# Per-head sums of the recurrent layer: sixteen 64x64-stationary products on four quarters of the array in place of four 128x128-stationary ones

## The chip, the cores and the metric

One core of a Trainium2 chip runs the whole program. The metric is the device time of one execution in microseconds (us). The engines work side by side, each through its own list of instructions in a fixed order: TensorE (PE in the profile; its weight loads are PEld), VectorE (DVE), ScalarE (ACT), GpSimd (POOL) and SyncE (SP, which here only issues DMAs). An instruction whose input is not ready holds up everything behind it on its engine.

## The reference, cut to what matters

The program is two layers over 512 tokens of width 1024. The first has an RWKV-7 time mixer with 12 heads of 64 channels beside a cross-attention into 256 memory tokens; the second has chunked attention. Both end in a gated feed-forward part. Two places of the first layer need one number per token and head:

```
kk = k_h * per_head(k_k)
kk = kk / jnp.maximum(jnp.sqrt(jnp.sum(kk * kk, axis=-1, keepdims=True)), 1e-12)
...
y = wkv7_scan(r_h, w_h, k_h, v_h, -kk, kk * a_h)
mean = jnp.mean(y, axis=-1, keepdims=True)
var = jnp.mean(jnp.square(y - mean), axis=-1, keepdims=True)
y = (y - mean) * lax.rsqrt(var + LN_X_EPS) * per_head(lnx_w) + per_head(lnx_b)
```

The sum runs over the 64 channels of a head. Everything is float32.

## The kernel before, in words

Tensors lie transposed: channels on the 128 partitions, 512 tokens along the free axis. The 12 heads are worked on as 6 pairs, one head on partitions 0 to 63 (`HS[0]`), the other on 64 to 127 (`HS[1]`). A pair `i` passes through three generators:

- `prepare(i)` projects keys, queries and values with products against weight tiles (the helper `dense`, lines L241, L242 and L245: the high and low parts of activations by `whi`, then `wlo`). Its inner generator `keys()` squares the keys, calls the helper for the norm, multiplies (L1195 to L1204 build the tiles `AR` and `KB`), forms the scores (L1210), copies them to `Lc` (L1215) and sends them through DRAM (L1218, L1224) to `Lr`, from which a triangular solver on DVE (L1233 to L1246) works.
- `front(i)` and `back(i)` turn the scores into the state recursion and the outputs, mostly with small products of 64 or 32 rows (L1300, L1324, L1326, L1358, L1375, L1418, L1434, L1445, L1453, L1462, L1467, L1472). `back` calls the helper for the output norm.

The helper is `head_rsqrt`. It is called by `keys()` for pairs 0, 1, 4 and 5 and by `back` for pairs 0, 3, 4 and 5, eight calls in all; the other pairs use `head_wide`, which is not touched. A call holds the squares `sq` (128 channels by 512 tokens) stationary in four pieces of 128x128 and passes the two columns of `sel` through them (L1082). `sel` has a column for each head, with zeros in the other head's rows. So each piece yields 128 tokens by 2 heads in one PSUM bank. DVE then adds or clamps a constant (`fix`, its line is that of the caller: L1192 for keys, L1487 for outputs), takes ten small steps of a reciprocal root (`rsqrt_steps`, L280 to L284), spreads the result (L1088), and PE turns it back (L1091).

The generators of several pairs, the memory keys and values of both layers (`mem_kv`, products L241 to L245 with 256 columns, and L1060 to L1062) and other work are woven into one program by `weave`: it takes the next step from the generator that is furthest behind, by the cost in ns that each step yields. A scheduler then orders each engine's list with its own estimates of durations. So a yielded cost or the number of instructions can change the order of instructions that the diff does not touch. Weight tiles come in by SP (L214 into `wraw`, two buffers), ACT makes `whi` (L195) and DVE or a DMA the rest `wlo` (L203, three buffers each).

Small products share four PSUM banks that are handed out in turn (`ps_s`); the memory products have two others (`psl`) and the projections two more (`psd`).

Of the kernel before, what the change touches and what calls it, by code (L numbers as in the profile page):

```python
# [18 lines left out]
P = 128  # L19
# [102 lines left out]
def trunk_kernel(ctx, tc, A, out):  # L122
    nc = tc.nc
    PE, V, SC, GP = nc.tensor, nc.vector, nc.scalar, nc.gpsimd
# [34 lines left out]
    def C(name, lo=0, n=None):  # L159
        o, w = COFF[name]  # L160
        return cst[:, o + lo:o + lo + (w if n is None else n)]
# [23 lines left out]
    def tmp(dt=F32, shape=(P, S)):  # L185
        return banks["tmp"].tile(list(shape), dt, name="tmp", tag="tmp")
# [43 lines left out]
    def behind_dense():  # L230
        return tc.issue_after(dense_at[0].ins)
# [45 lines left out]
    def rsqrt_steps(pool, a, n):  # L277
        r = pool.tile([P, 8], F32, name="rsq", tag="rsq")
        q = pool.tile([P, 8], F32, name="rsq2", tag="rsq2")
        V.tensor_scalar(r[:, :n].bitcast(I32), a.bitcast(I32), -0.5, 1597463007.0, op0=ALU.mult, op1=ALU.add)  # L280
        for _ in range(3):
            V.tensor_tensor(q[:, :n], r[:, :n], r[:, :n], op=ALU.mult)
            V.scalar_tensor_tensor(q[:, :n], q[:, :n], -0.5, a, op0=ALU.mult, op1=ALU.mult)
            V.scalar_tensor_tensor(r[:, :n], q[:, :n], 1.5, r[:, :n], op0=ALU.add, op1=ALU.mult)  # L284
        return r
# [603 lines left out]
    HS = (top, bot)  # L889
# [24 lines left out]
    def kt_(name, shape=(P, S), bufs=None, dt=F32):  # L914
        if bufs is None:
            return kp.tile(list(shape), dt, name=name, tag=name)
        return kp.tile(list(shape), dt, name=name, tag=name, bufs=bufs)
# [72 lines left out]
    with tc.issue_after(last_x[0].ins), tc.issue_after(last_x[1].ins):  # L990
        lw = next(ls)
        kw = split_w(kraw[:], 1024)
        for m in range(KD):
            sq = acc if m == 0 else tmp()
# [78 lines left out]
        return ap.rearrange("p (c t) -> p c t", c=NCH)  # L1073

    I64 = COFF["i64"][0]

    def head_rsqrt(sq, sel, fix, bank, tied=False):

        ps = bank()
        with behind_dense() if tied else ExitStack():  # L1080
            for t in range(4):
                PE.matmul(ps[:, 2 * t:2 * t + 2], sq[:, t * P:(t + 1) * P], C(sel), start=True, stop=True)  # L1082
        a = kt_("hra", (P, 8), bufs=2)
        fix(a[:], ps[:, 0:8])
        r = rsqrt_steps(kp, a[:], 8)
        yield 700, 3000
        bc = tmp()
        V.tensor_copy(bc[:].rearrange("p (g c) -> p g c", c=64), r[:].unsqueeze(2).to_broadcast([P, 8, 64]))  # L1088
        pt = bank()
        for t in range(4):  # L1090
            PE.transpose(pt[:, t * P:(t + 1) * P], bc[:, t * P:(t + 1) * P], C("ident"))  # L1091
        yield pt
# [33 lines left out]
    def prepare(i, T):  # L1126
# [57 lines left out]
        def keys():  # L1184
            k = T["k"]
            SC.activation(kn[:], k[:], AF.Copy, scale=kneg[:, i:i + 1])
            if i in WIDE_K:
                hr = head_wide(kn[:], lambda o, p: V.tensor_scalar(o, p, 1e-24, None, op0=ALU.max), ps_s, i < NPAIR - 1)
            else:
                sq = tmp()  # L1190
                SC.activation(sq[:], kn[:], AF.Square)
                hr = head_rsqrt(sq, "hs1", lambda o, p: V.tensor_scalar(o, p, 1e-24, None, op0=ALU.max), ps_s, i < NPAIR - 1)  # L1192
# [97 lines left out]
    def front(i, T, nxt=None):  # L1290
# [19 lines left out]
        def rows_kb():  # L1310
            ps = [ups(), ups()]
            for c in range(8):
                for h in range(2):
                    PE.transpose(ps[h][:, c], KB[HS[h], c, 1 - h:3 - h].rearrange("p s t -> p (s t)"),
                                 cst[HS[h], I64:I64 + 64])
            for h in range(2):
# [3 lines left out]
        def rows_av():  # L1320
            ps = [ups(), ups()]
            for c in range(8):
                for h in range(2):
                    PE.matmul(ps[h][HS[h], c], AR[HS[h], c, 0], cst[HS[h], I64:I64 + 64], start=True, stop=True)  # L1324
                for h in range(2):
# [74 lines left out]
    def back(i, T, dst, tiles=own_tiles, go=None):  # L1400
# [85 lines left out]
        if i not in WIDE_Y:  # L1486
            hr = head_rsqrt(sq, "hsm", lambda o, p: V.tensor_scalar(o, p, LN_X_EPS, None, op0=ALU.add), ps_s)  # L1487
# [71 lines left out]
    with tc.issue_after(norm_at[0].ins):  # L1559
        for m in range(KD):  # L1560
            sq = macc[:, :NMEM] if m == 0 else tmp()[:, :NMEM]
# [470 lines left out]
```

## Time and profile before

| What | Value |
|---|---|
| Median of 3 runs | 1292.26 us (1291.12 to 1293.33) |
| Span of the profiled execution | 1292.6 us |
| PE busy | 1260.9 us, 98% |
| DVE busy | 1031.7 us |
| ACT busy | 846.4 us |
| Products of the changed line | 64 records, 8.2 us busy together |
| PE's idle time between 45 and 345 us | 9.1 us |

The profile page lists no time of the profiled execution other than its span. The span lies 0.3 us above the median of the runs and within them, so differences worked out on it are taken over to the median unchanged. Each float32 product of the small kind appears as two records (two passes), so 32 products of the changed line are 64 records. A row of the timeline gives start, duration, engine, line, operation, output and inputs, shape and count; a square bracket says how long the engine stood idle before it and who released it. The recurrent layer's head work lies between about 45 and 350 us; what comes behind it is in the same order in both kernels.

### The profile page before, as it was taken

The numbers are of one execution on the slowest core, as the hardware profiler recorded it, in microseconds if no ns is written. First come the engines' busy times: TensorE is split into PE (matmuls) and PEld (weight loads), VectorE is DVE, ScalarE is ACT, GpSimd is POOL, SyncE is SP. The second block draws the span as 40 slices with busy tenths as digits, with TensorE's granted clock in tenths as the row PEclk, the third lists the DMA queues.
The fourth block names the chain that finished last, engine by engine and source line by source line (L and its number), as shares of the span: only waits on it lengthen the run. The fifth ranks groups of instructions, "written<-read, shape, count | busy, mean of one in ns | idle before, by whom it ended". The sixth has DMA issues, their size and how long they took to land.

```text
span 1292.6 us, 26432 instructions
## 1 busy us (share of the span) xinstructions
PE 1260.9 (98%) x10420; PEld 1083.1 (84%) x10420; DVE 1031.7 (80%) x1956; ACT 846.4 (65%) x1398; POOL 152.7 (12%) x182
## 2 busy tenths in 40 slices
PE   9999999999999999999999999999999999999997
PEld 7887777777789999998888878787789999998886
DVE  7867677765688999998876876658889999998684
ACT  6566767856476777776554676757757777765662
POOL 1000000000001222320220000000002222211200
PEclk9999999999999999999999999999999999999999
DMA  5364444453055988996984322234429989978951
GB/s 204 110 174 106 100 96 89 92 109 96 30 166 126 212 198 198 206 208 172 274 185 122 118 87 82 76 104 123 130 61 212 197 193 211 208 161 262 233 149 66
DMA packets 95581, 192.14 MB, mean 149 GB/s; under 512 B 22112, under 2 KB 30432, under 8 KB 95456
## 3 DMA queue, kind: packets, MB, share of 16 engines
q1 hardware_dynamic: 68592, 129.14, 31.9%
q0 software_dynamic: 26864, 61.31, 27.3%
q8 instruction: 82, 1.34, 0.4%
q14 instruction: 43, 0.35, 0.1%
HBM read 174.20 MB, written 6.29 MB: 140 GB/s over the span
## 4 chain that ended last, share of the span: by engine, by line
PE 62%; DVE 15%; ACT 8%; DMA 8%; issue 6%; SPq 0%; POOL 0%; ACTq 0%; DVEq 0%; POOLq 0%
PE psf L434 8%; PE psf L698 7%; PE psd L245 6%; PE psd L241 5%; PE psd L242 5%; DMA wlv<-in_ffn_in_dram 4%; PE psf L436 4%; PE psf L703 4%; PE psd L698 3%; ACT whi L499 2%; DMA wraw<-in_ffn_in_dram 2%; PE psd L703 2%; DVE raw L486 1%; PE pss L1817 1%; DVE wlo L504 1%
## 5 line engine op out<-in xcount | busy, mean ns | idle before, releaser
L499 ACT CAST whi<-raw 128x1024 fp32r<-128x1024 f32 (+1 forms) x168 | 153.3, 942 | 62.3 <-PE psf L434 29.5
L434 PE MATMUL psf<-th,whi 128*128 128x256 f32 x672 | 161.4, 278 | 2.5 <-ACT tmp L553 1.9
L434 PE MATMUL psf<-tl,whi 128*128 128x256 f32 x672 | 161.1, 276 | 0.0
L195 ACT CAST whi<-wraw 128x1024 fp32r<-128x1024 f32 x84 | 87.6, 1048 | 78.3 <-PE psd L242 37.4
L434 PEld LDWEIGHTS psf<-th,whi 128*128 128x128 f32 x672 | 125.8, 188 | 3.9 <-ACT tmp L553 2.9
L434 PEld LDWEIGHTS psf<-tl,whi 128*128 128x128 f32 x672 | 126.0, 188 | 0.0
L504 DVE TENSOR_TENSOR wlo<-raw,whi 128x1024 fp32r<-128x1024 f32 (+1 forms) x108 | 109.3, 1012 | 9.1 <-ACT whi L499 8.9
L241 PE MATMUL psd<-r1h,whi 128*128 128x512 f32 x264 | 107.4, 408 | 0.0
L242 PE MATMUL psd<-r1l,whi 128*128 128x512 f32 x264 | 105.0, 398 | 0.0
L203 DVE TENSOR_TENSOR wlo<-wraw,whi 128x1024 fp32r<-128x1024 f32 x65 | 79.2, 1219 | 22.3 <-ACT whi L195 20.4
L688 ACT CAST whi<-raw 128x1024 fp32r<-128x1024 f32 (+1 forms) x52 | 49.6, 954 | 59.9 <-PE psf L698 33.1
L689 DVE TENSOR_TENSOR wlo<-raw,whi 128x1024 fp32r<-128x1024 f32 (+1 forms) x52 | 56.5, 1097 | 38.9 <-ACT whi L688 31.5
L436 PE MATMUL psf<-th,wlo 128*128 128x256 f32 x504 | 78.0, 276 | 0.0
L245 PE MATMUL psd<-r1h,wlo 128*128 128x512 f32 x264 | 74.3, 403 | 0.6 <-DMA wlo<-in_ffn_in_dram 0.4
L471 POOL DMA_DIRECT2D wlv<-in_ffn_in_dram x40 | 60.7, 1516 | 59.5 <-DVE tmp L572 59.1
L436 PEld LDWEIGHTS psf<-th,wlo 128*128 128x128 f32 x504 | 66.8, 188 | 0.0
L434 PE MATMUL psf<-r2h,whi 128*128 128x256 f32 x252 | 60.9, 278 | 0.7 <-ACT whi L499 0.7
L434 PE MATMUL psf<-r1h,whi 128*128 128x256 f32 x252 | 60.7, 277 | 0.7 <-ACT whi L499 0.7
L434 PE MATMUL psf<-r2l,whi 128*128 128x256 f32 x252 | 60.7, 277 | 0.0
L434 PE MATMUL psf<-r1l,whi 128*128 128x256 f32 x252 | 60.6, 277 | 0.0
L241 PEld LDWEIGHTS psd<-r1h,whi 128*128 128x128 f32 x264 | 49.6, 188 | 12.0 <-issue 2.1
L525 ACT ACTIVATE tmp<-tmp,vec 128x512 f32<-128x512 f32 x44 | 36.0, 817 | 33.3 <-DVE tmp L512 33.3
(611 smaller groups left out, 3576.8 us busy)
## 6 DMA issues: line engine op xcount, KB each, us to landing
raw<-in_ffn_in_dram SPq DMA_DIRECT2D x42, 512.0 KB, 5.2
raw<-in_ffn_in_dram SPq DMA_DIRECT2D x84, 256.0 KB, 5.5
wlv<-in_ffn_in_dram POOLq DMA_DIRECT2D x40, 512.0 KB, 8.6
raw<-in_ffn_out_dram SPq DMA_DIRECT2D x30, 512.0 KB, 6.2
raw<-in_ffn_out_dram POOLq DMA_DIRECT2D x24, 512.0 KB, 8.4
wraw<-in_wA_dram SPq DMA_DIRECT2D x20, 512.0 KB, 4.1
wraw<-in_w_out_dram SPq DMA_DIRECT2D x16, 512.0 KB, 4.1
wraw<-in_ffn_outp_dram SPq DMA_DIRECT2D x16, 512.0 KB, 4.5
```

The lines of the kernel that those rows point to most:

```text
L195: high = lambda: pin(SC.copy(hi[:, :n], raw))
L203: pin(V.tensor_tensor(lo[:, :n], raw, hi[:, :n], op=ALU.subtract))
L241: PE.matmul(ps, wh[:, j * P:(j + 1) * P], ah, start=start and n == 0, stop=False)
L242: dense_at[0] = PE.matmul(ps, wh[:, j * P:(j + 1) * P], al, start=False, stop=False)
L245: dense_at[0] = PE.matmul(ps, wl[:, j * P:(j + 1) * P], act(k)[0], start=False, stop=stop and n == len(ks) - 1)
L434: PE.matmul(ps, wh[:, o + k * P:o + k * P + P], x[k][n], start=k == n == 0, stop=False)
L436: PE.matmul(ps, wl[:, ol + k * P:ol + k * P + P], x[k][0], start=False, stop=k == 3)
L471: GP.dma_start(self.low[:].rearrange("p (a s) -> p a s", a=2), self.second, accum_op=ALU.add)
L499: keep(SC.copy(hi[:, :n], self.pair(what) if n > S else self.raw[:, what]))
L504: keep(V.tensor_tensor(lo[:, :n], self.pair(what) if n > S else self.raw[:, what], hi[:, :n], op=ALU.subtract))
L698: PE.matmul(ps[:], a[:, k0 + i, ts], hi[:, i * S:i * S + S], start=bool(first) and (first is True or t in first) and a is act[0] and i == ...
L703: PE.matmul(ps[:], act[0][:, k0 + i, ts], lo[:, i * S:i * S + S], start=False, stop=bool(last) and t in last and i == n - 1)
```

## The change: what it does

Each piece of squares is cut into four 64x64 blocks: two heads by two halves of 64 tokens. For each, one product with 64 rows and 64 columns stationary, on its own quarter of the array, takes the place of a quarter of a 128x128 product. The head's rows go to a bank of their own, so a call takes two of the four shared banks in place of one, and `fix` is run twice, on four columns each. The cost that the step yields to `weave` goes from 700 to 400.

```
+    QUADS = ((0, 0), (1, 1), (0, 1), (1, 0))
     def head_rsqrt(sq, sel, fix, bank, tied=False):
-        ps = bank()
+        ps = [bank() for _ in range(2)]
         with behind_dense() if tied else ExitStack():
             for t in range(4):
-                PE.matmul(ps[:, 2 * t:2 * t + 2], sq[:, t * P:(t + 1) * P], C(sel), start=True, stop=True)
+                for h, n in QUADS:
+                    PE.matmul(ps[h][HS[n], 2 * t:2 * t + 2], sq[HS[h], t * P + n * 64:t * P + n * 64 + 64],
+                              C(sel)[HS[h]], start=True, stop=True)
         a = kt_("hra", (P, 8), bufs=2)
-        fix(a[:], ps[:, 0:8])
+        for h in range(2):
+            fix(a[:, h::2], ps[h][:, h:8:2])
         r = rsqrt_steps(kp, a[:], 8)
-        yield 700, 3000
+        yield 400, 3000
```

PE has 32 products less of one kind and 128 more of the other; DVE has 8 instructions more. Lines from L1085 on carry a number 4 higher in the new file (L1210 becomes L1214, L1195 becomes L1199). The order of the engines' lists is the same up to the first call and again from about 350 us on. In between most rows keep their places. The largest move is right behind the first call, where pair 0 and the memory keys and values are woven together.

On DVE, behind the first call's norm: `kn`, `AR` and `KB` are pair 0's keys, `kh` its scaled keys, `wlo` the low part of a weight tile, `psd_478` the finished query projection. Before:

```order
L1050 TENSOR_TENSOR kmT0_87<-psl_565,W_140 128x256
L1195 TENSOR_TENSOR kn_333<-kn_333,pss_634 128x512
L1050 TENSOR_TENSOR kmT0_87<-psl_603,W_140 128x256
L1196 TENSOR_TENSOR AR_331<-kn_333,E_93 128x8x64
L1198 SCALAR_TENSOR_TENSOR tmp_641<-a_326,kn_333 128x512
L203 TENSOR_TENSOR wlo_656<-wraw_653,whi_655 128x1024
L1200 SCALAR_TENSOR_TENSOR KB_330<-tmp_641,Ei_329 128x8x64
L1203 TENSOR_TENSOR kh_334<-krv_469,tmp_644 128x512
L1160 TENSOR_TENSOR tmp_665<-psd_478,rho_71 128x512
L1204 TENSOR_TENSOR KB_330<-kh_334,Ei_329 128x8x64
```

The same place on DVE after:

```order
L1050 TENSOR_TENSOR kmT0_87<-psl_579,W_140 128x256
L1199 TENSOR_TENSOR kn_333<-kn_333,pss_646 128x512
L1050 TENSOR_TENSOR kmT0_87<-psl_617,W_140 128x256
L1200 TENSOR_TENSOR AR_331<-kn_333,E_93 128x8x64
L1202 SCALAR_TENSOR_TENSOR tmp_653<-a_326,kn_333 128x512
L1164 TENSOR_TENSOR tmp_664<-psd_478,rho_71 128x512
L1204 SCALAR_TENSOR_TENSOR KB_330<-tmp_653,Ei_329 128x8x64
L1207 TENSOR_TENSOR kh_334<-krv_469,tmp_656 128x512
L1167 SCALAR_TENSOR_TENSOR krv_666<-tmp_664,vec_67,krv_666 128x511
L1208 TENSOR_TENSOR KB_330<-kh_334,Ei_329 128x8x64
L203 TENSOR_TENSOR wlo_678<-wraw_675,whi_677 128x1024
```

The weight tile's low part stood in the middle of the key chain and now stands behind its end; the query projection's read has moved up into the chain.

On PE at the same place: `psd_670` is pair 0's value projection, `psl_651` and `psl_652` the first layer's memory values, L1062 the products that need that low part. Before:

```order
L245 MATMUL psd_670<-r1h_68,wlo_475 128x512 x2
L1062 MATMUL psl_651<-wlo_656,ML_138 128x256
L1062 MATMUL psl_652<-wlo_656,ML_138 128x256
L1060 MATMUL psl_651<-whi_655,ML_138 128x256
L1061 MATMUL psl_651<-whi_655,ML_139 128x256
```

The same place on PE after:

```order
L1061 MATMUL psl_674<-whi_677,ML_139 128x256
L245 MATMUL psd_669<-r1h_68,wlo_475 128x512 x2
L1214 MATMUL pss_721<-KB_330,AR_331 64x64 x16
L1062 MATMUL psl_673<-wlo_678,ML_138 128x256
L1062 MATMUL psl_674<-wlo_678,ML_138 128x256
```

Pair 0's scores (L1210, now L1214), which came 32 products later, now come right behind the value projection and ahead of L1062.

On SP's queue at the same place: the weight tiles of the second layer's memory keys (`in_w_memk`) and values (`in_w_memv`), and the eight small transfers of the scores. Before:

```order
L214 DMA wraw_816<-in_w_memk_dram 128x1024
L214 DMA wraw_865<-in_w_memk_dram 128x1024
L214 DMA wraw_912<-in_w_memv_dram 128x1024
L1218 DMA d1_731<-Lc_730 16x8x16 x8
L214 DMA wraw_946<-in_w_memv_dram 128x1024
L1224 DMA Lr_745<-d1_731 32x256 x4
```

The same place on SP after:

```order
L214 DMA wraw_830<-in_w_memk_dram 128x1024
L1222 DMA d1_739<-Lc_738 16x8x16 x8
L214 DMA wraw_881<-in_w_memk_dram 128x1024
L1228 DMA Lr_753<-d1_739 32x256 x4
L214 DMA wraw_926<-in_w_memv_dram 128x1024
L214 DMA wraw_960<-in_w_memv_dram 128x1024
```

The scores' eight transfers have moved ahead of two weight tiles and `Lr` ahead of two more, one place each past the next.

## Prediction

> **What bounds the kernel now.** I read, in this order, the page's first line, a table of stages, the group of the changed line, the timeline around its calls, and the waits of PE.
>
> ```profile
> PE 1260.9 (98%) x10420; PEld 1083.1 (84%) x10420; DVE 1031.7 (80%) x1956; ACT 846.4 (65%) x1398; POOL 152.7 (12%) x182
> 45.00:100.00 55.00, 52.36 (x441) 45.85 (x439) 40.86 (x110) 31.21 (x48) 1.86 (x2) 0.97 0.57 156
> 100.00:345.00 245.00, 238.54 (x3705) 180.81 (x3705) 171.25 (x492) 164.22 (x346) 12.88 (x15) 1.00 0.40 88
> 345.00:1292.60 947.60, 926.72 (x6101) 823.19 (x6099) 782.91 (x1283) 619.31 (x950) 134.41 (x146) 1.00 0.65 163
> L1082 PE MATMUL pss<-cst,tmp 128*128 128x2 f32 x64 | 8.2, 250 | 0.8 <-ACT tmp L1482 0.6 <-ACT tmp L1191 0.2
> ```
>
> The last three columns of a stage are the granted clock, the DMA share and GB/s. PE is busy 52.4 of 55.0 and 238.5 of 245.0 us in the two stages that hold the calls, so a microsecond of PE's work saved there is worth up to a microsecond, and a microsecond for which PE is made to wait costs one. The third stage is untouched in order. The changed line holds 8.2 us of overlapping durations in the whole program; what a call occupies is read from starts.
>
> **A call's own time.** Start of the first product to start of the next other product, in the first call and in the fourth:
>
> ```profile
> 47.55 1.05 PE L1082 MATMUL pss<-cst,tmp 128*128 128x2 f32 x8 [0.17 <-ACT tmp L1191]
> 48.47 0.59 PE L311 MATMUL pss<-cst,W 128*128 128x2 f32 x4
> ...
> 220.28 1.05 PE L1082 MATMUL pss<-cst,tmp 128*128 128x2 f32 x8
> 221.26 1.15 PE L1462 MATMUL psl<-ML,VT 128*64 128x64 f32 x32
> ```
>
> 0.92 and 0.98 us for 8 records, 115 to 122 ns each, with two columns moving. The changed call has 32 records of 64x64. Two patterns of such products stand in the trace: L1324 with L1326, whose order over the quarters is that of `QUADS`, and L1210, which changes quarter differently.
>
> ```profile
> 90.71 0.39 PE L241 MATMUL psd<-r1h,whi 128*128 128x512 f32 x1
> 90.94 0.39 PE L242 MATMUL psd<-r1l,whi 128*128 128x512 f32 x1
> 91.25 0.27 PE L1324 MATMUL pss<-cst,AR 64*64 64x64 f32 x2
> ...
> 92.19 0.22 PE L1326 MATMUL pss<-cst,v 64*64 64x64 f32 x2
> 92.35 0.50 PE L241 MATMUL psd<-r1h,whi 128*128 128x512 f32 x1
> ...
> 65.45 1.15 PE L1210 MATMUL pss<-KB,AR 64*64 64x64 f32 x32
> 66.53 0.39 PE L1060 MATMUL psl<-whi,ML 128*128 128x256 f32 x1
> ```
>
> The first pattern passes 64 records in 92.35 - 91.25 = 1.10 us, the last two of them 0.16 us ahead of the next dense product; the other 62 take 0.94, or 15 ns each. 30 such records and a last pair give 0.45 + 0.16 = 0.61. Entering from dense products takes 0.31 (90.94 to 91.25) where a dense one follows in 0.23, so 0.08 more than the old call paid: I take 0.65. The gain is 0.27 to 0.33 a call, **0.29 by the first call's neighbours, 8 x 0.29 = 2.3 us**. Bounds: at the pace of L1210, 32 records in 1.08 us, a call loses 0.10 to 0.16 (8 x 0.16 = 1.3 lost); if the two ends cost nothing, 32 x 15 ns = 0.48 and 8 x 0.50 = 4.0 are gained.
>
> The Trainium skill (TensorEngine Tiling (Array Packing), section Key Properties) says that a change of tiling mode drains TensorE first, which speaks against the change since every call now has two. The rows agree: 0.31 against 0.23 on the way in, 0.16 against 15 ns on the way out. By a sum that left the drain out the calls would bring 4.0 us, by the sum above 2.3.
>
> **What the second bank and the second `fix` add.**
>
> ```profile
> 219.75 0.69 DVE L1454 TENSOR_TENSOR VT<-pss,dE 128x512 f32<-128x512 f32 x1 [0.85 <-PE pss L1453]
> 221.37 0.17 DVE L1192 TENSOR_SCALAR hra<-pss 128x8 f32<-128x8 f32 x1 [0.93 <-PE pss L1082]
> ...
> PE pss L1091 <- DVE tmp L1088: 0.4, 2, 0.2
> ```
>
> With four shared banks a call takes the one that comes free next too. In the fourth call that is one which L1454 reads until 219.75 + 0.69 = 220.44, 0.16 after the old call's start: **+0.15**. Elsewhere I see no late reader and take 0 (up to 0.15 for each of the other seven calls, 1.05). The eight extra `fix` instructions lengthen a chain by 0.17 us each; DVE is idle often enough (80% busy) and PE has dense work meanwhile, except where it already waits for that chain: twice, 0.4 us. So 2 x 0.17 = **+0.3** (bounds 0 and 8 x 0.17 = 1.4).
>
> **The moved instructions behind the first call.** Here the lists change most, and here PE waits today:
>
> ```profile
> 59.49 0.63 PE L245 MATMUL psd<-r1h,wlo 128*128 128x512 f32 x2
> 61.49 0.50 PE L1062 MATMUL psl<-wlo,ML 128*128 128x256 f32 x2 [1.37 <-DVE wlo L203]
> 69.01 0.38 PE L241 MATMUL psl<-ML,whi 128*128 128x256 f32 x1 [0.79 <-ACT vm L1065]
> ...
> 71.98 0.29 PE L241 MATMUL psl<-ML,whi 128*128 128x256 f32 x1
> ...
> 58.94 0.68 DVE L1198 SCALAR_TENSOR_TENSOR tmp<-a,kn 128x512 f32<-128x512 f32 x1
> 60.22 1.23 DVE L203 TENSOR_TENSOR wlo<-wraw,whi 128x1024 fp32r<-128x1024 f32 x1 [0.59 <-ACT tmp L1202]
> 61.36 0.68 DVE L1200 SCALAR_TENSOR_TENSOR KB<-tmp,Ei 128x512 f32<-128x512 f32 x1
> 61.96 0.68 DVE L1203 TENSOR_TENSOR kh<-krv,tmp 128x512 f32<-128x512 f32 x1
> 62.56 0.68 DVE L1160 TENSOR_TENSOR tmp<-psd,rho 128x512 f32<-128x512 f32 x1
> 63.17 0.68 DVE L1204 TENSOR_TENSOR KB<-kh,Ei 128x512 f32<-128x512 f32 x1
> ```
>
> Each of the 128x512 rows on DVE takes 0.6 from start to start. After the change, with all 0.29 earlier: L1198 starts at 58.65, the projection's read and the first `KB` follow, `KB` is written at 58.65 + 3 x 0.6 = 60.45. The value projection's last product ends near 60.12 - 0.29 = 59.8, and the scores stand right behind it: PE waits 0.65. The scores take 1.08 (row of L1210) and end at 61.5. L203 now stands behind `kh`, the row of L1167 and the second `KB`: 60.45 + 3 x 0.6 = 62.25, and 1.22 more is 63.5, when L1062 can start. Before, it started at 61.49, with the scores' 1.08 still to come: an equivalent 62.57. So PE is 0.9 later here although the call saved 0.29: **+1.2**. The wait of 0.79 at 69.01 was for an ACT row held up by the copies of the scores, which now come long before it: **-0.8**.
>
> Further on, the weight tile for the memory values is split behind the solver's first rows and one read, which it preceded:
>
> ```profile
> 76.78 1.23 DVE L203 TENSOR_TENSOR wlo<-wraw,whi 128x1024 fp32r<-128x1024 f32 x1 [1.29 <-ACT whi L195]
> 77.92 0.36 DVE L1233 TENSOR_TENSOR Xu<-Lr,cst 128x120 f32<-128x120 f32 x1
> 78.79 0.28 DVE L1235 TENSOR_TENSOR Xsa<-cst,Xu 128x120 f32<-128x120 f32 x1
> 79.11 0.80 DVE L1239 SCALAR_TENSOR_TENSOR Xsa<-Lr,Xsa 128x14 f32<-128x14 f32 x5
> ```
>
> That is 0.36 + 0.28 + 0.80 + 0.68 = 2.12 us of work put in front. DVE's idle 1.29 us takes up 1.29 of it at the most, if the scores are back by then: PE waits between 0.8 and 2.1 longer, and I take the middle, **+1.5**. The four loose fragments of L1300 that the new order makes cost an entry of 0.08 each: **+0.3**. The stretch comes to 1.2 - 0.8 + 1.5 + 0.3 = **+2.2 us**; its bounds are -0.8 (all new waits hidden) and 1.2 + 2.1 + 0.3 + 0.8 = 4.4 (the old wait stays too).
>
> **Sum:** -2.3 + 0.15 + 0.3 + 2.2 = +0.35. The profiled execution of before has its span alone, 1292.6, 0.3 above the median 1292.26. On the median: **1292.6 us**.
>
> **Rivals.** *Slower, by SP's queue.* The scores' eight issues now stand ahead of the second layer's second weight tile of memory keys.
>
> ```profile
> 66.93 1.52 ACT L1215 COPY Lc<-pss 32x256 f32<-32x256 f32 x4
> ...
> 67.31 4.27 SPq L1218 DMA_DIRECT2D d<-Lc  x8
> ...
> wraw<-in_w_memk_dram SPq DMA_DIRECT2D x4, 512.0 KB, 3.6
> ...
> 65.18 1.05 ACT L195 CAST whi<-wraw 128x1024 fp32r<-128x1024 f32 x1 [0.66 <-DMA wraw<-in_w_memk_dram]
> 66.50:69.90 3.40, 2.61 (x23) 2.38 (x20) 1.71 (x3) 3.30 (x9) 0.00 (x0) 1.00 0.44 145
> ```
>
> Scores done at 61.5 put the issues at 62 to 66.3, the tile at 69.9, its cast at 71.0. In the trace of before the products with this tile begin at 71.98; with -0.8 + 0.9 that is 72.1. The margin is 1.1 us. ACT is busy 3.30 of 3.40 us around its copies; should it make them as late as before (66.9), the issues end at 71.6, the tile is cast at 76.3 and PE stands 4.2 us; from 1.1 us of delay on, each microsecond counts. With 3 us lost the time is 1295.6. Against it: ACT has little to do at 61.5 to 63.
>
> *Faster, by the clock.* PE runs at half the clock for 3.4 us right behind the first call:
>
> ```profile
> 46.40:49.80 3.40, 2.96 (x23) 2.78 (x24) 3.40 (x10) 1.25 (x3) 0.00 (x0) 1.00 0.51 140
> 49.80:53.20 3.40, 3.40 (x18) 3.40 (x17) 3.30 (x24) 2.11 (x3) 0.00 (x0) 0.50 0.35 136
> ```
>
> The stretch before holds 0.17 us of idle time at the call and 0.92 us of products that load much and move two columns. With the call shorter, dense products move up into it; if the drop then fails to come, half of 3.4 us, 1.7, is gained. With the waits behind the call only changing places (0 for 2.2), -2.3 + 0.45 - 1.7 = -3.5: 1288.7. Against it: the gap of a little stretch is all that changes, and the waits are worked out row by row. The Trainium skill (TensorE: Matmul & The Clock Gate, section Part 1: The HAM clock gate) has a free-running window of 3413 ns, after an idle one of which the clock halves. The 3.4 us agree; a PE busy 2.96 of 3.40 before the drop does not look idle.
>
> *The change doesn't do what it says:* the quarters don't overlap with two columns moving, and 32 records take 1.08 as L1210's do. Then +1.3 + 0.45 + 2.2 = +3.9: 1296.2. For it: no products of two columns on quarters stand in the trace. Against it: L1324 and L1326 go over the quarters in the order of `QUADS` and pass 64 columns, 32 times as many, at 15 ns a record.
>
> **How the numbers follow.** The forecast, no more than 0.2% (2.6 us, about what a measurement of this kernel can tell from no change) to either side, 0.66; SP's queue 0.13; the clock with hidden waits 0.15; quarters in a row 0.06. Bounds of the terms within the forecast: calls that gain up to 4.0 in place of 2.3 and a stretch of 0 in place of 2.2 give 1292.6 - 3.9 = 1288.7; the stretch at 4.4 gives 1294.8. The range leaves out the far parts: **1289.3 to 1295.6**. Faster 0.17 (the clock, and a little of the forecast's tail), slower 0.18 (the queue, the quarters), the same 0.65.
>
> **What the profile after would show.** Groups L1084 and L1085 in about 0.65 us a call, 15 ns from start to start inside; two `fix` rows of 0.17; PE waiting for `KB` at 59.8 and for `wlo` L203 until 63.5; no wait for `vm` at 69; a new wait for `wlo` around 78 to 81; the half-clock stretch still at 49.8. Wrong would be a call near 1.1 us, a wait for the second tile of memory keys above a microsecond, a changed clock, or moves between 100 and 345 us (PE idle there now 6.5 us) that I took to cost nothing: cover for these is PE's own queue of dense products, and without it each costs up to the 0.6 of a DVE row.

## The result: 8 to 11 us slower

The changed kernel takes 1300.78 us (median of 4, 1297.87 to 1305.28) against 1292.61 (4 runs), a ratio of 1.0069 with the interval 1.0045 to 1.0093. The forecast was 1292.6 with 1289.3 to 1295.6. Run again (e1_again below) it took 1302.66 against 1291.74, 1.0081 (1.0061 to 1.0101): 8.2 and 10.9 us more. Its times scatter over 7 to 9 us, those of before over 2 to 6.

The first lines of its page, its stages as they were shown of before (last three columns: granted clock, DMA share, GB/s), and three stretches at half the clock:

```profile
span 1303.5 us, 26825 instructions
PE 1267.1 (97%) x10612; PEld 1088.1 (83%) x10612; DVE 1032.7 (79%) x1964; ACT 845.9 (65%) x1398; POOL 153.1 (12%) x182
...
45.00:100.00 55.00, 51.66 (x480) 45.37 (x479) 38.84 (x101) 30.25 (x45) 1.86 (x2) 0.94 0.53 153
100.00:345.00 245.00, 236.37 (x3785) 178.98 (x3785) 167.15 (x483) 159.93 (x332) 12.90 (x15) 0.97 0.41 89
345.00:1303.50 958.50, 936.33 (x6177) 830.68 (x6175) 790.48 (x1309) 624.31 (x966) 134.74 (x146) 1.00 0.64 161
63.78:67.19 3.41, 3.17 (x15) 3.17 (x16) 2.68 (x5) 1.91 (x4) 0.00 (x0) 0.50 0.15 17
278.82:292.47 13.65, 13.65 (x104) 9.54 (x105) 7.03 (x29) 5.15 (x10) 0.86 (x1) 0.50 0.31 66
418.77:422.18 3.41, 3.41 (x18) 3.41 (x17) 3.38 (x6) 2.66 (x4) 0.93 (x3) 0.50 0.62 101
```

PE's share of busy time is hardly lower; what is new is the clock, 0.97 in the stage from 100 to 345 us and 0.94 ahead of it, where it was 1.00 and 0.97. Before, the only half-clock stretch ahead of the program's end was that of 3.4 us at 49.8 us. It is still there (50.1 us), and three more add 20.5 us at half the clock, worth up to 10 us where PE is the bound (an estimate: half of their length). Over the ten runs of this kernel the time falls with the mean clock, 0.987 to 0.997, by 0.9 us for each 0.001.

A second view puts each product's start beside the start of the same product before, both from the span's start. The shift is +0.4 us at 45 us and 0.15 behind the first call, +2.9 at 90 us, +2.0 at 160 falling to +0.7 at 270, **+8.8 at 285, +9.0 at 300**, +9.4 at 400, **+13.8 at 415**, and +10.9 at the end. So the loss comes in three steps: the moved instructions behind the first call, something between 270 and 300 us, and something at 410 us, in the order that the change did not touch.

The step at 270 us, on PE:

```profile
274.58 0.22 PE L1379 MATMUL pss<-Y,Tn 16*16 16x16 f32 x5
277.36 0.26 PE L1379 MATMUL pss<-Y,Tn 16*16 16x16 f32 x11 [2.57 <-issue]
...
270.00:275.00 5.00, 4.79 (x139) 3.66 (x140) 4.18 (x9) 4.34 (x11) 0.24 (x1) 1.00 0.97 202
275.00:277.40 2.40, 0.04 (x5) 0.04 (x8) 0.00 (x0) 1.36 (x3) 0.00 (x0) 1.00 0.43 48
...
q8 instruction: 83, 1.36, 0.4%
```

In the middle of a run of sixteen like products PE stands for 2.57 us, and "issue" says that no engine and no transfer of data kept it. The DMA engines are full (0.97) in the 5 us ahead. The last row, from the page's DMA queues, names transfers that no instruction of the kernel issues: queue q8 moves 83 packets in 1.36 MB, 16 KB each. Shared out over PE's 10,612 products and as many loads that is 64 bytes an instruction, so a packet would be 256 instructions of PE's program; the two numbers fit, since 83 pieces of 256 are just what those instructions need. In the trace one of them starts at 275.02, and PE goes on 2.34 us later.

That gives the theory tested below. **F:** PE's program comes in pieces of 256 instructions, and the place in the program where one piece ends and the next begins is called a border here. A piece is asked for when PE has passed the border before it. Asked for while weight tiles fill the DMA engines, it starts late; small products (two instructions, a load and a product, in some 15 ns) eat what is left, and PE runs dry. A PE that has stood can get half the clock for one to five stretches of 3.41 us. Its rivals: **O**, the new order itself costs the time; **C**, chance.

### The profile page after: what moved, and what is told of

Its sections match the earlier page's. It is cut to its first block, busy times and chain, and to the rows that moved or that the text cites. A ratio compares the mean times of both kernels' runs of the same rounds, so it can differ in the third digit from the quotient of the medians.

```text
span 1303.5 us, 26825 instructions
## 1 busy us (share of the span) xinstructions
PE 1267.1 (97%) x10612; PEld 1088.1 (83%) x10612; DVE 1032.7 (79%) x1964; ACT 845.9 (65%) x1398; POOL 153.1 (12%) x182
## 3 DMA queue, kind: packets, MB, share of 16 engines
q8 instruction: 83, 1.36, 0.4%
## 4 chain that ended last, share of the span: by engine, by line
PE 70%; DVE 12%; ACT 7%; issue 5%; DMA 4%; SPq 0%; ACTq 0%; POOL 0%; DVEq 0%; POOLq 0%
PE psf L434 12%; PE psf L698 7%; PE psf L436 6%; PE psd L245 6%; PE psd L241 5%; PE psd L242 5%; PE psf L703 4%; PE psd L698 3%; PE psd L703 2%; PE pss L1821 1%; ACT whi L499 1%; DMA raw<-in_ffn_in_dram 1%; DMA wraw<-in_ffn_in_dram 1%; DVE raw L486 1%; PE pss L698 1%
## 5 line engine op out<-in xcount | busy, mean ns | idle before, releaser
L241 PEld LDWEIGHTS psd<-r1h,whi 128*128 128x128 f32 x264 | 50.1, 190 | 12.0 <-issue 2.1
```

The lines of the kernel that those rows point to most:

```text
L241: PE.matmul(ps, wh[:, j * P:(j + 1) * P], ah, start=start and n == 0, stop=False)
```

## The experiments

All times are medians, in us, with the runs of before on the same chip beside them; the clock is the median of the runs.

**The changed kernel again** (no edit).

> The changed kernel once more, nothing edited. Theory F (fetch and clock): PE runs out of code behind 1 MB of weight tiles, near 275 us in its profile, since the 60 more products ahead of that place shift where its code is read in pieces; the idle PE then gets half the clock for several stretches of 3.4 us. By F the stall near 275 us (2.57 us) and the half-clock stretch behind it (13.65 us) are there again, within a microsecond or two, and the time is 1297 to 1305. Theory C (chance): stalls and half-clock stretches fall anywhere in any kernel; then they are at other places now, and the time may be 1292 to 1305. Theory O (order): only the waits of 0.84 and 1.76 us near 61 us belong to the change, 1293 to 1296, and what lies above was one bad execution.

Measured 1302.66 (1299.19 to 1307.99), clock 0.993, before 1291.74 and 0.998. The profiled run stood 0.90 us at 232.5 us for "issue", with 3.41 us at half the clock from 235.5, and not at 275; then it waited 4.02 us at 406.9, with 6.83 us at half the clock. The stop at 232.5 stands at the same instruction as one of 0.81 us at 234.7 in the first profile; the long one at 275 did not come again, and the larger part of this profile's loss (6.4 us of the shift) is the step at 410 us. So the loss repeats and its place only in part: F's claim of the same place was wrong, and some chance is in it.

**Quads without the new order.**

```diff
-        yield 400, 3000
+        yield 700, 3000
```

> The sixteen products a call, but the old cost of 700 in the step, which puts pair 0's scores and the split of the weight tile back into the old order: no waits of 0.84 and 1.76 us near 61 us. Theory F: the calls gain 8 x 0.33 = 2.6 us, the first stretch costs nothing, but the code has the same length as in the changed kernel, so the stall near 275 us and the half clock behind it stay: 1290 + 2.5 + up to 7, or 1293 to 1300. Theory O: 1290 (1292.3 - 2.6), no stall. Theory C: 1290 on most runs, single ones up to 1300.

1296.84 (1293.89 to 1300.64), ratio 1.0038 (1.0021 to 1.0055). The waits at 61 us are those of before (1.37), the shift against before gets 1.8 us better from 60 to 220 us as calls gain, and 1.04 us of "issue" at 229.8 us with half the clock at 231.4 give it back. PE then waits 3.75 us at 404.4: the step at 410 us again, and most of what this profile loses. By the medians, half of the slowdown is there with the old order.

**The new order without quads.**

```diff
 # kernel before
-        yield 700, 3000
+        yield 400, 3000
```

> The old 128x128 products with the new cost of 400: the changed kernel's order behind the first call with the old code length. Theory F: the waits near 61 us cost 2.0 to 2.6 us, no stall near 275 us: 1294 to 1295. Theory O, if the new order is what costs everything: 1299 to 1303. Theory C: 1294 on most runs, single ones up to 1302.

1300.86 (1297.57 to 1302.19), 1.0059 (1.0043 to 1.0074), clock 0.992. F's 1294 to 1295 is missed by 6. The profile has the waits at 61 us and a shift of 2.3 us behind them, and then this:

```profile
274.62 0.27 PE L1375 MATMUL pss<-Y,Tn 16*16 16x16 f32 x14
276.18 0.20 PE L1375 MATMUL pss<-Y,Tn 16*16 16x16 f32 x2 [1.29 <-issue]
```

with 13.65 us at half the clock from 278.5. With the old number of instructions PE still stopped for "issue": the new order has L1210, L1358 and L1467 in other places around 270 us, and there the transfer of the same piece of code, which before began at 265.98, ahead of the burst of weight tiles, began at 273.92, behind it. So the order alone, too, can decide whether a piece comes ahead of a burst of weight tiles or behind it.

**Four tiny products in front of the changed kernel.**

```diff
     for _ in range(6):
         PE.matmul(idle[:, 0:256], zeros[:, 0:P], zeros[:, 0:256], start=True, stop=True)
+    # and 4 of 64x64 with 2 columns
```

> The changed kernel with four tiny products (64x64, 2 columns) added behind the six warm-up products at the program's start, 16 instructions of PE. With the 240 that the five calls ahead of 275 us add, this makes 256, one whole piece of code, so that piece borders lie there as they did before the change. Nothing else moves; the four cost at most 0.4 us. Theory F: no stall near 275 us and no half clock behind it: 1292.5 to 1295, that is 6 to 8 below the changed kernel. Theories C and O: the same as the changed kernel beside it, within its own scatter, with the stall as often as there.

1308.91 (1306.07 to 1313.09), 1.013 (1.011 to 1.0151), clock 0.987: 6 us more for four tiny products, the contrary of what F was made to say. Its profile:

```profile
235.68 0.53 PE L1379 MATMUL pss<-Y,Tn 16*16 16x16 f32 x40 [3.07 <-issue]
```

and 1.44 us more at 276.4, 1.83 at 318.3, with 17 us at half the clock behind the first two. The alignment had been worked out for one place and the old order. At 230 us the shift was 192 + 16 and not 256.

To see whether PE really stops at borders, count the instructions that it had done when it stopped (loads, products and the semaphore waits between them), between 100 and 345 us, in all sixteen profiles of this study. Of its idle times over 0.5 us there, those that other engines end (0.5 to 0.9 us, nearly the same ones in every kernel) fall at any count. The 21 others have "issue" as their cause, and each falls at a count of 449 + 256 n exactly. Those over 1.2 us (the last column is the time from the start of the transfer until PE went on):

```
kernel               stop at  length  done   n    code transfer began   PE went on after
after                 274.8    2.57   6849   25         275.02               2.34
e3_sums400            274.9    1.30   6593   24         273.92               2.26
e4_after_pad4         232.6    3.07   5569   20         233.24               2.44
e4_after_pad4         276.4    1.44   6849   25         275.21               2.59
e4_after_pad4         318.3    1.83   8129   30         317.86               2.23
e7_quads700_aligned   292.7    1.60   7617   28         292.10               2.19
e9_before_pad48       235.6    1.28   5569   20         234.47               2.41
e10_sums400_pad16     311.5    1.75   7873   29         311.04               2.21
e11_after_pad16       232.3    1.30   5569   20         231.38               2.21
e11_after_pad16       309.9    1.50   8129   30         309.27               2.18
e12_four_calls        229.3    1.55   5569   20         228.53               2.33
```

All 21 end 2.2 to 2.7 us after a 16 KB transfer of q8 began. They lie at five places, near 107, 233, 276, 293 and 310 to 318 us, in bursts of small products. Stops at any place, as C has it, would not all fall on borders. The kernel before (two profiles) and e5_before_pad60 and e6_before_pad64 below have none; every other kernel has one to three. The Trainium skill (Runtime: NRT & Kernel Launch, section Instruction fetch mechanics) says that an engine's instructions are refilled in 16 KiB blocks of 256 while it runs, at a cost that is mostly hidden. The blocks agree; the cost is up to 3.07 us here (e4_after_pad4), where a piece comes behind a burst of weight tiles.

**Borders moved in the kernel before**, whose order stays: 4 of the 6 warm-up products and 62 tiny ones (240 instructions more), or 66 (256 more), or 50 (192 more).

> The kernel before, with two of the six warm-up products replaced by 62 tiny ones (64x64, 2 columns), 240 more PE instructions ahead of everything: as many as the changed kernel has ahead of 275 us. Order, sums and PE's other work are those of before. The tiny ones cost some 2 to 6 us at the start, read off in the trace as the shift at 50 us. Theory F (code in pieces of 256 instructions, read late when weight tiles move): the border of a piece is crossed inside the burst of weight tiles near 230 us and again near 270 us, so PE stands near 233 us for up to 1 us and near 275 us for 1 to 2.5 us, with 0 to 4 half-clock stretches of 1.7 us behind them: 3 to 8 us more than e6_before_pad64. Theory O (order): the same time as e6_before_pad64, no stalls. Theory C (chance): the same distribution as e6_before_pad64.

> As e5_before_pad60 with four tiny products more, 256 instructions, so one whole piece of code: borders lie at the same instructions as before the change. Same cost at the start within 0.3 us. Theory F: no stall at 233 or 275 us; the time is that of before plus the shift at 50 us (2 to 6 us). Theories O and C: the same as e5_before_pad60.

> The kernel before with two warm-up products replaced by 50 tiny ones, 192 more PE instructions at the start, the number that the changed kernel has ahead of 230 us. Order and sums of before; the start costs some 4 us as in e5_before_pad60 and e6_before_pad64 (1295.7 and 1296.5). Theory F: the border of a piece now falls into the dense products during the burst of weight tiles before 230 us, so PE runs dry in the second run of L1375 near 237 us (0.5 to 3 us), and again near 279 us (about 1 us); with half-clock stretches behind them 1297 to 1305. Theory C or O: like those two kernels, 1295 to 1297, no stall near 237 us.

1295.71 (1294.01 to 1299.32), 1296.49 (1292.96 to 1299.14) and 1300.10 (1291.78 to 1305.39). The first two are alike, against F's 3 to 8 us between them: here F failed in the time. With 240 more a piece's transfer begins just ahead of the burst near 230 us, and near 279 us PE stands 0.2 us at the count 6849, not 1 to 2.5. With 256 there is no stop, as forecast. With 192 both stops came where they were expected, the first after the count 5569:

```profile
235.32 0.28 PE L1472 MATMUL psl<-MQ,W 64*64 64x64 f32 x3
236.88 0.21 PE L1472 MATMUL psl<-MQ,W 64*64 64x64 f32 x1 [1.28 <-issue]
...
229.00:234.50 5.50, 5.50 (x122) 4.07 (x118) 5.05 (x11) 2.80 (x6) 0.20 (x1) 1.00 0.92 195
```

and the second 0.91 us at 279.5. The stops follow the borders; the medians, 4 us apart, can't be put down to them alone, since the tiny products in front don't cost the same each time: ahead of 45 us the profiled runs of these three are 6.5, 4.1 and 4.1 us late, and that of the next is 1.8 us late. **Again, unchanged:**

> e9_before_pad48 once more, unchanged. Theory F: the stall near 235.6 us and the smaller one near 279.5 us stand at the same instructions again, 0.8 to 1.5 and 0.5 to 1.5 us, with 0 to 4 half-clock stretches behind them; 1297 to 1303. Theory C (chance): other places.

1296.83 (1293.01 to 1306.62): 1.03 us at 233.4 (its start was 2 us earlier) and 0.65 at 275.7, the same instructions, and no half clock behind them in that run. So the stops repeat and the clock's answer does not. The scatter of 14 us goes with the clock: the fastest of the ten runs had 0.998, the slowest 0.988. Against the second kernel's 1296.49 this run shows no difference in the median.

**Half a burst.** The weight tile that POOL reads at 228.3 us is made by DVE instead, in the kernel with 192 more.

```diff
-            if src is not None:
+            nth[0] += src is not None
+            if src is not None and nth[0] != 12:
```

> The kernel before with 192 PE instructions more at the start (e9_before_pad48, 1300.1, which stood 1.28 us at 235.6 us where its code ran out), and one weight tile's low part, the one that POOL reads from DRAM at 228.3 us, is made by DVE instead (L203, 1.22 us). So the burst of transfers there is 512 KB and not 1 MB; DVE and PE keep their order up to the stall but for one product. Theory F (the code is read late since weight tiles fill the DMA engines): the read that began at 234.47 begins by 232.5, 1 to 2 us before PE needs it, the stall at 235.6 us is 0 to 0.3 us, no half clock behind it; 2 to 4 us below the kernel beside it. Rival R (PE itself asks late, since it waits for semaphores): the read still begins near 234.5 and the stall stays at 1 to 1.5 us.

```profile
236.13 0.28 PE L1472 MATMUL psl<-MQ,W 64*64 64x64 f32 x4
236.34 0.37 PE L1375 MATMUL pss<-Y,Tn 16*16 16x16 f32 x30
...
229.00:232.70 3.70, 3.70 (x44) 2.90 (x44) 3.67 (x7) 1.60 (x2) 0.00 (x0) 1.00 0.44 142
```

The code's transfer began at 232.75 and not at 234.47; at the count 5569, in the first row, PE goes on without a stop. With half the tiles ahead of it the transfer came earlier and the stop was gone, as F said; R, that PE asks late, is not what held it here. This is one profile. The total didn't follow: 1300.30 (1297.62 to 1301.94) against 1296.83 beside it. The profiled run had the stop at 277.0 (0.91) still, and the order behind 240 us differs in other rows as well, so its total isn't explained.

**Borders moved in the two kernels with the new order**, 16 tiny products in front.

> The old sums with the cost of 400 (e3_sums400, 1300.9) and 16 tiny products at the start, 64 PE instructions. Same order on every engine as e3_sums400. Theory F: the border that PE crossed at the start of the burst of weight tiles near 270 us is now crossed some 2 us earlier, so the stall of 1.3 us and the 13.65 us at half clock behind it go: 1291.4 + 2.2 (first stretch) + 0.4 (start) = 1294, 1293 to 1296. Theory O (the order itself costs) and C: 1301 as e3_sums400.

> The changed kernel with 16 tiny products at the start, same order on every engine: 256 more PE instructions than before the change near 230 us, 304 near 275 us. Theory F: the stalls near 233 and 275 us go, one like that of e7_quads700_aligned near 293 us (1.6 us) stays: 1293 to 1298, some 5 to 10 below the changed kernel (1302.7) and more below the one with 4 tiny products (1308.9). Theories O and C: 1301 to 1304, as the changed kernel.

The second came out in F's range: 1297.51 (1294.29 to 1310.96), 5 below the changed kernel with more work to do, and no stop at 275; but against F it has one of 1.30 us at 232.3, and another of 1.50 at 309.9. The first lost its stop at 275 as expected and yet took 1303.37 (1301.14 to 1308.47), since the next border moved into another burst:

```profile
310.70 0.80 PE L1462 MATMUL psl<-ML,VT 128*64 128x64 f32 x20
313.25 0.57 PE L1462 MATMUL psl<-ML,VT 128*64 128x64 f32 x12 [1.75 <-issue]
...
314.71:331.78 17.07, 17.07 (x176) 13.59 (x176) 7.52 (x19) 7.10 (x24) 0.00 (x0) 0.50 0.11 32
```

1.75 us of stop are followed by 17.07 us at half the clock, 8.5 us of work: the shift against before grows from 1.8 at 300 us to 11.3 at 320.

**Quads with the borders laid out by hand**, old order: 16 tiny products in front and the last call doubled, or quads in four calls alone.

```diff
-                for h, n in QUADS:
+                for h, n in QUADS * (2 if again[0] == 8 else 1):   # e7
...
+        ps = [bank() for _ in range(2 if again[0] < 5 else 1)]     # e12, old sums from the fifth call on
```

> The sixteen products a call with the cost of 700, 16 tiny products at the start and the last call's sums made twice (the result is the same): with the calls' own 192, 240 and 384 instructions the shift of the code is 256 near 230 us, 304 near 275 us and 512 behind the last call, that is 0, 48 and 0 past whole pieces. Theory F: no stall of a microsecond at 230 or 275 us; 1292 - 2.6 (calls) + 0.5 to 1.5 (start) + 0.5 (doubled call), 1290 to 1292, 4 to 6 below the same kernel without the additions (1296.8). Theories O and C: about 1 above that kernel, 1297 to 1299.

> Sixteen products in the first four calls alone, cost 700, 16 tiny products at the start: 256 more PE instructions than before the change from the fourth call to the end, one whole piece. Theory F: no stall of a microsecond, 1291.4 - 4 x 0.33 + 0.4 = 1290.5, 1289.5 to 1291.5, so level with before or a little below. Theories O and C: 1294 to 1297, as e2_quads700 and e7_quads700_aligned.

The first took 1294.71 (1291.45 to 1297.23), 1.0022 (1.0012 to 1.0032): 2 below e2_quads700, without its stop at 230, but with one that had not been thought of, 1.60 us at 292.7, and above F's 1290 to 1292. The second took 1292.83 (1289.58 to 1298.01), 1.0011 (0.9998 to 1.0023): level with before, above F's 1289.5 to 1291.5, and still

```profile
230.86 0.36 PE L1385 MATMUL pss<-Y,Tn 16*16 16x16 f32 x25 [1.55 <-issue]
```

where a whole piece of shift should have kept the old borders. Its code transfer began at 228.53, e7's for the same piece at 222.75; the order up to there is not quite that of before, and what made one ask ahead of the burst and the other behind it stays open. No version beat the kernel before.

**The kernel before again.**

> The kernel before, nothing edited, one more profile. Theory F: no stall over 0.5 us at 230 to 235 or 270 to 280 us, no half-clock stretch there, 1291 to 1293. Theory C: stalls and half-clock stretches like those of the changed kernel are as likely here, and it would show one or more.

1290.57, no stop at any border, no half clock ahead of the end:

```profile
100.00:345.00 245.00, 239.21 (x3707) 180.66 (x3706) 171.55 (x494) 164.53 (x346) 12.03 (x14) 1.00 0.39 88
```

The 23 timed runs of before on one chip lie between 1289.38 and 1295.47. The kernel before is one whose borders happen to fall well: with them moved by 192 instructions the same kernel stops (e9_before_pad48).

## Why the prediction was wrong

*A call's own time.* Right, with a better size:

```profile
48.06 0.64 PE L1084 MATMUL pss<-cst,tmp 64*64 64x2 f32 x32 [0.23 <-ACT tmp L1195]
48.63 0.61 PE L311 MATMUL pss<-cst,W 128*128 128x2 f32 x4
```

0.57 us, forecast 0.65; the gain is 0.35, 0.34, 0.34, 0.19 and 0.31 in the first five calls. The fourth, with the late bank, takes 0.79 (0.65 + 0.15 forecast). The 0.3 for the second `fix` did not come: no wait of PE for that chain is left. The rival of quarters that don't overlap falls. The prediction's citation of the Trainium skill (TensorEngine Tiling (Array Packing), section Key Properties), that a change of mode drains TensorE, agrees with this: 0.57 against the 0.48 of a sum without switches.

*The first stretch.* Right in the rows, and its total partly by luck:

```profile
60.29 0.68 DVE L1204 SCALAR_TENSOR_TENSOR KB<-tmp,Ei 128x512 f32<-128x512 f32 x1
62.75 2.35 DVE L203 TENSOR_TENSOR wlo<-wraw,whi 128x1024 fp32r<-128x1024 f32 x2
...
61.12 1.15 PE L1214 MATMUL pss<-KB,AR 64*64 64x64 f32 x32 [0.84 <-DVE KB L1204]
64.02 0.80 PE L1062 MATMUL psl<-wlo,ML 128*128 128x256 f32 x2 [1.76 <-DVE wlo L203]
```

This execution runs 0.4 us behind that of before from its start, so L1062 stands at 63.6 on the old scale, forecast 63.5. The wait of 0.79 for `vm` is gone. The wait for the later weight tile was forecast at 0.8 to 2.1; it is 0.94 in e1_again and below 0.25 here. In all the shift grows by 2.8 us here and by 2.3 with the old sums in the new order (e3_sums400), forecast 2.2. That the totals come so near is luck: both profiles lack the wait that 1.5 of the forecast stood for, and both have 3.41 us at half the clock from 63.8 or 63.5 us, which no term had. Where no half clock falls there, the shift grows by 2.1 (e1_again, with the wait) and 1.1 (e11_after_pad16, without it). The rival by SP's queue did not come.

*The step that failed* is a sentence at the end: "moves between 100 and 345 us ... that I took to cost nothing: cover for these is PE's own queue of dense products, and without it each costs up to the 0.6 of a DVE row". No dense product covers an instruction that PE doesn't have yet. The sum entered both causes of that at 0. It counted the 128 small products as time on the array, at 15 ns a record, and never as instructions that have to be read: 96 products more in all, in two passes with a load each, or 384. And it priced a moved row by the rows of DVE beside it, never by where PE's code then arrives: e3_sums400, with moved rows and not one product more, has a stop of 1.29 us with 13.65 us at half the clock behind it and is 9.1 us slower. Between 100 and 345 us the shift grows from 2.6 to 9.2 us in the profiled run, by way of two stops (0.81 and 2.57 us) and the clock. "The third stage is untouched in order" was entered at 0 as well, and 4.4 us were lost there at 410 us (below).

*The clock* was a rival with the wrong sign. The prediction looked for a half-clock stretch to go (1.7 us gained) and gave none a chance to come. The stretch at 49.8 was no mark of the calls either: it is missing in the profiles of e1_again, e2_quads700 and of the kernel before, taken again. The Trainium skill (TensorE: Matmul & The Clock Gate, section Part 1: The HAM clock gate) has the clock halved after an idle window of some 3.4 us and full again after a busy one. Here a stop of 1.29 us among small products was followed by half the clock (e3_sums400), and the row of 278.82 to 292.47 shows PE busy all the time and at half the clock for four windows. By that row, being busy in the profile was not enough to bring the clock back.

The stops and the clock belong together: the sixteen profiles have twelve half-clock stretches between 100 and 345 us, and each begins during one of the 21 stops or at most 2.4 us behind its end. Nine of the stops, of up to 1.83 us, have none behind them; what decides it is not known.

*What stays open.* The step at 410 us, in a stretch whose order is that of before:

```profile
417.16 0.63 ACT L476 ACTIVATE wlo<-raw 128x512 fp32r<-128x512 f32 x1 [3.65 <-DMA raw<-in_ffn_in_dram]
...
PE psf L434 <- ACT tmp L553: 4.7, 2, 3.0
```

A weight tile issued by SP lands 7.3 us after its issue, and not 5.1, where SP's issue ahead of it took 1.07 us and not 0.46, so that it was issued 1.05 us behind POOL's tile and not 0.43. Three profiles have it (this one, e1_again, e2_quads700); in the others PE waits there for less than 1 us. The traces tell what sets these three apart: in them a 16 KB transfer of PE's code begins 0.18 to 0.27 us ahead of the slow issue (L457), in the thirteen others at least 1 us ahead of it, and the issue takes 0.46 us. Over all sixteen traces, the 56 issues of L457 that start less than 0.5 us after such a transfer began all took more than 0.7 us; of the 950 that start 2 us or more after one, 10 did. With the borders moved, the step is gone (e4_after_pad4 and e11_after_pad16 for the changed kernel, e7_quads700_aligned for e2_quads700). So the place of the borders decides this step too, as far as these traces tell, by slowing SP's issue and not by PE running out of code; no experiment was aimed at it.

It is not settled how the 8 to 11 us share out between count and order: alone they cost 5.1 (e2_quads700) and 9.1 (e3_sums400), together 10.9 on the same chip. That doesn't add up; both acting through the same borders would explain it, but no run separates them there.

One reading of the start needs mending: the runs list a time 1.8 us above each execution's span, so the profiled execution of before (span 1292.6) was one of 1294.4, 2 us above its median, and not 0.3. The forecast's base, the median, is not touched by this.

## What to carry to other kernels

Count the instructions of an engine as well as their time: many small products in place of a few large ones move every piece of code behind them, and where a border meets a burst of weight tiles PE can run dry. Look for "issue" in the waits and for clock below 1.00 in a table of stages before explaining a loss by the instructions that were edited. A change worth 2 us in a kernel whose parts lie this close has to be timed with the code shifted by a few amounts, since 16 instructions in front moved the changed kernel's median by 6 us.

## What the runs showed of the hardware that was not expected

- PE's code arrives in 16 KB pieces on a queue of its own. In the 21 stops PE goes on 2.2 to 2.7 us after the start of a piece's transfer; behind a burst of weight tiles one started 6 us later than before, on the kernel's own scale (e3_sums400).
- A stop of 1.3 to 2.6 us can be followed by 13.65 to 17.07 us at half the clock; others of 1.50 (e11_after_pad16) and 1.83 us (e4_after_pad4) are followed by none.
- An issue of SP's (L457) takes 0.46 us, and 1.07 to 1.31 us where a transfer of PE's code has begun less than 0.3 us ahead of it (the three profiles with the step at 410 us).
- With four products of 64x64 and 2 columns more at its start, the changed kernel took 6 us longer (1308.91 against 1302.66).
